# Two-layer hybrid diffusion trunk: the latent query rows of the first two head pairs ahead of the key and query rows of the last two

## The chip, the cores and the metric

The kernel runs on one core of one Trainium2 chip. The metric is the device time of one execution in microseconds (us); lower is better. The core has TensorE (PE, matrix products, with its weight loads PEld), VectorE (DVE), ScalarE (ACT), GpSimd (POOL) and SyncE (SP), which issues the transfers of this kernel. PSUM is the memory that TensorE writes, SBUF the working memory; weights and inputs come from the chip's main memory.

## The reference

Two layers work on 640 tokens: 512 latent ones and 128 context ones. In each layer the modulated input goes through one input projection, whose columns feed three mixers side by side; one output projection merges them, and a SwiGLU channel mixer follows. Cut to what matters here, for the latent tokens:

```python
proj = einsum("bsd,de->bse", h, w_in)
a_x, a_b, a_c, d_q, d_k, d_v, m_cq, m_ckv, m_kpe = split(proj, offs)

y_a = a_b * short_conv(a_c * a_x, conv_w)

sc = einsum("bhmqd,bhmkd->bhmqk", q, k_all) * DIFF_SCALE     # 4 heads, 2 maps each
p  = softmax(sc);  a = p[:, :, 0] - lam * p[:, :, 1]
o_b = rms_norm(a @ v_all, diff_norm_w) * (1 - lam_init)

cq  = rms_norm(m_cq, q_norm_w)                # 384 wide
ckv = rms_norm(m_ckv, kv_norm_w)              # 256 wide
qc  = cq @ w_uq                               # 8 heads: 64 without and 32 with rotation
kv  = ckv_all @ w_ukv                         # 8 heads: 64 of key, 64 of value
k_m = concat([kv[..., :64], kpe_all]);  q_m = concat([q_nope, q_pe])
o_c = softmax(q_m @ k_m.T * MLA_SCALE) @ kv[..., 64:]

y = concat([y_a, y_b, y_c]) @ w_out
```

Latent tokens attend to 512 latent and 128 cached keys, context tokens to the 128 context keys. The keys, values and compressed latents of the context are outputs too.

## The kernel before

Activations lie with features on the partitions and the 640 tokens along the free axis. Every matrix product of the projections is made in three passes: operands are split into a rounded part `hi` and a remainder `lo`, and `matmul3` (L349 in the profile) adds hi by hi, hi by lo and lo by hi. Each 128-row weight block is loaded by SyncE into a staging tile `stg`, and split by ScalarE (L138, cast) and VectorE (L140, subtraction) into one of four weight tiles `wu`; the next split begins when an earlier block is given back (`W.done`). The order of the blocks is fixed by `plan`, from `WIN` for the input projection and from `JOBS` for the latent products.

A layer runs through `stage_in` (the input projection, one job per 128 output rows, in the order of `WIN`, ending with cq0, cq1 and cq2), `attention` (the latent projections and both attentions), the output projection and the channel mixer.

*Jobs.* `attention` walks through `JOBS` in order. `k0` to `k3` (`k_job`, L1131) make the latent key rows of head pairs 0 to 3, 12 matmuls each, and store them to the scratch tensors `kd` and `pd` by three DMAs. `v0` to `v5` (`v_job`) make the values of six key tiles, 6 matmuls each. `e0` and `e1` (`qpe_job`) make the rotated query rows of four heads each, `q0` to `q3` (`q_job`, L1154) the other query rows of a head pair, 18 matmuls each, stored to `qd` and `pd`. k and v jobs read the normalised key latent `ckvn`, e and q jobs the normalised query latent `cq`. A head pair's tiles come together in main memory: `load_pair(p)` (L1174) issues nine DMAs that read the 96 rows of each of the two heads back as `mq` and `mk` (hi and lo), and the context part `p32`.

*Score steps.* `plan_steps` (L1382) lists 64 score steps per layer. The first 32 are the differential attention: two head groups by two halves of the queries by eight steps of one map. The last 32 are the latent attention: four head pairs by two halves by four steps. A step is one call of `scores` (L1188): the matmuls (L1194), VectorE's row maximum `nm` (L1198), ScalarE's exponential `P` with its sum (L1209), VectorE's reciprocal, and GpSimd's scaling (L1228, L1248) or VectorE's weighted difference (L1232). Some steps later the transposes (L1269) and value products (L1280) of the unit follow, one key tile at a time. `STEPS` says how many steps are run in and behind each job of the input projection, and `JSTEPS` for each latent job: a pair is (steps in the middle of the job, steps behind it). `self.g` counts the steps, and other work is hung on the count: `LOADS` gives the counts at which `load_pair(0)` to `load_pair(3)` are issued, `SIDE` and `ASM` place the context attention, the norms and the differential tiles. Steps that no job takes run after the last one, with the latent steps, in the stage "tr".

*Buffers.* In the stage "score", from job dq1 to the end of the latent jobs, PSUM holds two tiles "mm" for projections and one tile "sc" for scores. In the stage "tr", scores use the "mm" tiles and two tiles "trx" take transposes. The probability tile of a step is chosen by `PAT` (for step numbers below `CKS`) or `PATC`: "P" is a pool of 6 that exists only inside `attention` (before that such a tile comes from the shared pool), "t" the shared pool of 31 tiles of 128 by 640, "c" the pool "ck" of 5 that also holds `ckvn`. The shared pool also holds `mk`, `mq`, the differential tiles `dqp` and `dkp`, `cq` and all passing tiles of the k, e and q jobs.

*Deferred work.* The normalisation of `cq` (`norm_cq` L967, `rms_later` L798) is counted in jobs: its statistics (L805, then ten small VectorE instructions) are written behind the third job from cq2 on, its broadcast (L815), the products (L975) and the splits (L836, L837) two jobs later.

```python
for (kind, j), n in zip(JOBS, JSTEPS):
    n = n if isinstance(n, tuple) else (0, n)
    self.mid, n = n
    if kind == "v":
        n += self.mid
    kinds[kind](l, int(j))
    self.tick()
    self.step(n)
```

The program is laid out by a scheduler that places instructions by the written order and by its own timing of when they can run, takes a free buffer for each new tile, and fixes the order on each engine. On the chip each engine follows that order.

Of the kernel before, what the change touches and what calls it, by code (L numbers as in the profile page):

```python
# [54 lines left out]
OUTI = 4  # L55
ADV = 0
HOLD = 2
LOADS = (29, 37, 43, 52)
SIDE = ((34, 37), (37, 40, 43), (36, 40), (47, 50, 56), (44, 47), (49, 51), (51, 54), (60, 62))
ADA_N = 12  # L60
ADA_IN = 1
# [3 lines left out]
ADA_FF2 = 1  # L65
ADA_LAG = 3
LAG = 4
STEPS = {"dv": (1, 2, 1, 1, 1), "ckv0": (0, 1), "ckv1": (0, 2), "ac1": (0, 2), "ab1": (0, 2), "cq0": (0, 2), "cq1": (0, 1), "dk1": (0, 0), "dq1": (0, 0)}
PAT = "PPPt"
PATC = "Pc"  # L70
CKS = 30
NP = 6
JOBS = "k0 k1 k2 k3 v0 v1 v2 v3 v4 e0 v5 e1 q0 q1 q2 q3".split()
JSTEPS = ((0, 1), (0, 1), (0, 1), (3, 0), (0, 1), (1, 0), (0, 0), (0, 0), (0, 1), (0, 2), (0, 0), (0, 0), (0, 1), (0, 0), (2, 1), (1, 0))
ASM = (9, 15)


# [121 lines left out]
class Trunk:  # L199
# [206 lines left out]
    def plan(self):  # L406
# [11 lines left out]
        for l in range(DEPTH):  # L418
# [8 lines left out]
            seen = []  # L427
            for kind, j in JOBS:
                key = {"k": ("uk", l, int(j) // 2), "v": ("uv", l), "e": ("uqpe", l), "q": ("uqn", l, int(j) // 2)}[kind]
# [550 lines left out]
    def dv_job(self, l):  # L980
# [8 lines left out]
        for j in (2, 0, 1, 3, 4):  # L989
# [18 lines left out]
            self.tick()  # L1008
            self.step(STEPS["dv"][j])

# [27 lines left out]
    def stage_in(self, l):  # L1038
# [41 lines left out]
        for n in names[nskew:]:  # L1080
# [4 lines left out]
            else:  # L1085
                u = self.W.get((n, l))
                mid, end = STEPS.get(n, (0, 0))
                ps = self.job(lambda k, p: u[:, p, 128 * k:128 * k + 128], h, NK, "AB", mid)
# [99 lines left out]
    def scores(self, pairs, qc):  # L1188
# [11 lines left out]
        n = self.np - 1  # L1200
        where = PAT[n % len(PAT)] if n < CKS else PATC[n % len(PATC)]
        if where == "c":
# [179 lines left out]
    def plan_steps(self, l):  # L1382
# [7 lines left out]
        def put(step, *fs):  # L1390
            self.after.setdefault(step, []).extend(fs)
# [35 lines left out]
        for g, i in enumerate(ASM):  # L1427
            put(i, lambda g=g: self.assemble_diff(1, 2 * g, 2 * g + 2))
        for p, i in enumerate(LOADS):
            put(i, lambda p=p: self.load_pair(p))  # L1430
# [20 lines left out]
    def attention(self, l):  # L1451
# [7 lines left out]
        kinds = {"k": self.k_job, "v": self.v_job, "e": self.qpe_job, "q": self.q_job}  # L1459
        for (kind, j), n in zip(JOBS, JSTEPS):  # L1460
            n = n if isinstance(n, tuple) else (0, n)
# [252 lines left out]
```

## Time and profile before

| | us |
|---|---|
| median of 3 runs | 1756.45 |
| lowest, highest | 1756.1, 1757.79 |
| profiled execution, its time | 1756.95 |
| its span in the trace | 1755.2 |
| TensorE busy | 1698.5 (97%) |
| VectorE, ScalarE, GpSimd busy | 975.0, 614.1, 247.7 |

The span is the time from the first to the last recorded instruction; the execution takes 1.75 us more. Busy time is the union of an engine's instructions; a busy TensorE can still work at a lower granted clock (1.00 is 2.4 GHz, 0.50 is 1.2 GHz). Layer 0's latent jobs run from about 184 to 238 us and its latent attention to about 350 us; layer 1's from about 1044 to 1098 us and to about 1199 us. A row of the timeline gives the start, the duration, the engine, the line, what is written and read, and in square brackets how long the engine stood idle before and what ended it. A row of the chain is a piece of the chain of work that ended last: start, duration, engine and line.

### The profile page before, as it was taken

To read this page: it belongs to the slowest core of one execution; us is meant where nothing else is said; L and a number is where in the kernel's file an instruction comes from. 1 tells how busy PE (TensorE), PEld (TensorE's weight loads), DVE (VectorE), ACT (ScalarE), POOL (GpSimd) and SP (SyncE) were. 2 spreads that over 40 slices of the span, in tenths; PEclk is the share of its full clock that TensorE was granted. 3 is DMA by queue.
4 is the path that set the end of the run, shared out by engine and by line. 5 is a ranking of instruction groups with operands and counts; after the bars stand their busy time and mean duration, and the time that the engine had idled before them with its cause. 6 is when DMAs were issued, how large, how long until landed. Compare 5 with 4: busy or idle time off the path is not lost.

```text
span 1755.2 us, 29477 instructions
## 1 busy us (share of the span) xinstructions
PE 1698.5 (97%) x11983; PEld 1589.4 (91%) x11983; DVE 975.0 (56%) x1824; ACT 614.1 (35%) x1046; POOL 247.7 (14%) x226
## 2 busy tenths in 40 slices
PE   7999989999999999999999999899999999999997
PEld 6998867698999999999999997678999999999997
DVE  3656777747466656756476668774652233232236
ACT  1334555524432122122245546553353212212221
POOL 0011113440001010101211111332200000000014
PEclk9999989999999999999999999899999999999998
DMA  9665584321355545545314634622212222222211
GB/s 323 210 208 142 169 252 139 119 89 51 94 153 151 156 126 145 174 133 146 107 52 148 217 121 157 173 76 75 73 61 77 81 72 73 73 78 78 68 53 60
DMA packets 100871, 217.38 MB, mean 124 GB/s; under 512 B 12160, under 2 KB 28928, under 8 KB 100736
## 3 DMA queue, kind: packets, MB, share of 16 engines
q1 hardware_dynamic: 100736, 215.50, 39.7%
q8 instruction: 94, 1.54, 0.4%
q14 instruction: 41, 0.34, 0.1%
HBM read 185.28 MB, written 30.18 MB: 123 GB/s over the span
## 4 chain that ended last, share of the span: by engine, by line
PE 86%; DVE 5%; ACT 3%; DMA 2%; issue 2%; POOL 0%; SPq 0%; POOLq 0%; ACTq 0%; DVEq 0%
PE mm L349 61%; PE mm L1194 4%; PE mm L372 4%; PE ac L1280 3%; PE mm L1513 3%; PE trx L1269 3%; PE mm L994 2%; PE mm L401 1%; DMA rawt<-in_w_ada 1%; ACT hv L781 1%; PE ac L476 1%; ACT wu L138 1%; DVE wu L140 1%; PE tr L449 1%; DMA mk<-kd 1%
## 5 line engine op out<-in xcount | busy, mean ns | idle before, releaser
L349 PE MATMUL mm<-h,wu 128*128 128x384 f32 (+1 forms) x4944 | 734.6, 309 | 1.8 <-ACT kp L908 1.5
L349 PEld LDWEIGHTS mm<-h,wu 128*128 128x128 f32 x4944 | 723.3, 188 | 8.7 <-issue 5.3
L138 ACT CAST wu<-stg 128x1024 fp32r<-128x1024 f32 (+2 forms) x200 | 201.5, 1011 | 686.1 <-PE mm L349 333.0
L140 DVE TENSOR_TENSOR wu<-stg,wu 128x1024 fp32r<-128x1024 f32 (+2 forms) x200 | 239.3, 1199 | 155.9 <-ACT wu L138 153.6
L349 PE MATMUL mm<-gh,wu 128*128 128x256 f32 (+1 forms) x1184 | 258.6, 309 | 0.0
L349 PEld LDWEIGHTS mm<-gh,wu 128*128 128x128 f32 x1184 | 198.7, 188 | 0.9 <-issue 0.6
L349 PE MATMUL mm<-gl,wu 128*128 128x384 f32 (+1 forms) x592 | 182.8, 309 | 0.0
L1198 DVE TENSOR_REDUCE nm<-mm 128x1 f32<-128x640 f32 x128 | 104.7, 818 | 50.4 <-PE mm L1194 49.6
L1547 DVE TENSOR_TENSOR gs<-gs,mm 128x640 f32<-128x640 f32 (+2 forms) x48 | 36.6, 763 | 154.2 <-PE mm L349 149.4
L668 DVE SCALAR_TENSOR_TENSOR x<-mm,ga,x 128x512 f32<-128x512 f32 x48 | 35.9, 749 | 145.6 <-PE mm L349 145.6
L349 PEld LDWEIGHTS mm<-gl,wu 128*128 128x128 f32 x592 | 111.4, 188 | 0.2 <-issue 0.2
L527 DVE SCALAR_TENSOR_TENSOR acc<-rawt,scT,acc 128x512 f32<-128x512 f32 x98 | 74.7, 763 | 60.4 <-DMA rawt<-in_w_ada 59.0
L372 PE MATMUL mm<-h,wu 128*128 128x384 f32 (+1 forms) x576 | 99.5, 331 | 7.4 <-ACT h L782 7.1
L372 PEld LDWEIGHTS mm<-h,wu 128*128 128x128 f32 x576 | 92.2, 205 | 12.6 <-ACT h L782 10.2
L349 PE MATMUL mm<-hi,wu 128*128 128x384 f32 (+1 forms) x400 | 89.9, 311 | 0.1
L687 POOL TENSOR_TENSOR accS<-x 128x640 f32<-128x640 f32 x4 | 9.9, 2488 | 507.3 <-DVE x L674 494.7
L1194 PE MATMUL mm<-mk,mq 96*128 96x384 f32 (+1 forms) x384 | 75.0, 336 | 5.2 <-ACT P L1209 2.4
L532 DVE SCALAR_TENSOR_TENSOR rawt<-rawt,scT 128x512 f32<-128x512 f32 x98 | 74.7, 762 | 2.1 <-POOL rawt L525 2.1
L1194 PEld LDWEIGHTS mm<-mk,mq 96*128 96x128 f32 x384 | 63.7, 200 | 12.3 <-ACT P L1209 5.2
L349 PEld LDWEIGHTS mm<-hi,wu 128*128 128x128 f32 x400 | 68.0, 188 | 2.6 <-issue 1.5
L1209 ACT ACTIVATE P<-mm,nm 128x640 f32<-128x640 f32 x56 | 44.6, 797 | 55.7 <-DVE nm L1198 45.0
L525 POOL TENSOR_SCALAR acc<-rawt,scT 128x512 f32<-128x512 f32 x14 | 9.8, 697 | 376.2 <-PE tr L542 376.1
(272 smaller groups left out, 2251.8 us busy)
## 6 DMA issues: line engine op xcount, KB each, us to landing
stg<-in_w_ff SPq DMA_DIRECT2D x104, 512.0 KB, 3.6
rawt<-in_w_ada SPq DMA_DIRECT2D x160, 256.0 KB, 3.1
stg<-in_w_in SPq DMA_DIRECT2D x30, 512.0 KB, 4.4
stg<-in_w_ff SPq DMA_DIRECT2D x32, 448.0 KB, 3.3
raw<-in_w_ada SPq DMA_DIRECT2D x32, 256.0 KB, 6.2
stg<-in_w_out SPq DMA_DIRECT2D x16, 512.0 KB, 4.4
mk<-kd SPq DMA_DIRECT2D x32, 240.0 KB, 5.8
mq<-qd SPq DMA_DIRECT2D x32, 192.0 KB, 5.4
```

Of the source, the lines that this page charges most:

```text
L138: nc.scalar.copy(u[:, 0, :ncol], t[:, :ncol])
L140: (nc.gpsimd if self.lo_pool else nc.vector).tensor_sub(u[:, 1, :ncol], t[:, :ncol], u[:, 0, :ncol].bitcast(F32))
L349: self.last = nc.tensor.matmul(out, w(k, pw), x(k, px), start=(k == 0 and i == 0), stop=(k == nk - 1 and i == 2)).ins
L372: self.last = nc.tensor.matmul(ps, u[:, pw, 128 * k:128 * k + 128], x(k, px)[:, c0:c1], start=(k == 0 and i == 0), stop=(k == NK - 1 and i ...
L527: nc.vector.scalar_tensor_tensor(self.acc[0], w, c[0], self.acc[0], ALU.mult, ALU.add)
L532: nc.vector.scalar_tensor_tensor(self.acc[1], w, c[1], self.acc[1], ALU.mult, ALU.add)
L1194: nc.tensor.matmul(ps[:, 128 + c0:128 + c1], q[:96, qc:qc + 128], k[:96, c0:c1], start=(i == 0), stop=(i == len(pairs) - 1))
L1198: nc.vector.tensor_reduce(nm, s, axis=AX.X, op=ALU.max, negate=True)
L1209: self.exp_end = nc.scalar.activation(P, s, AF.Exp, bias=nm, accum_out=sm).ins
L1269: nc.tensor.transpose(p[:, 256 * i + 128 * q:256 * i + 128 * q + 128], tiles[i, q][:, 128 * kt:128 * kt + 128], self.ident)
L1280: nc.tensor.matmul(acc[64 * i:64 * i + 64, :256], v(kt, i), hold[kt][:, 256 * i:256 * i + 256], start=(kt == 0), stop=(kt == 4))
L1513: self.last = self.nc.tensor.matmul(ps[:, c0:c1], u[:, pw, 128 * k:128 * k + 128], x(k, px)[:, c0:c1], start=(k == 0 and j == 0), stop=(k ...
```

## The change

Five constants change; no function does. The jobs are put in another order, with q0 and q1 ahead of k2, k3, q2 and q3, and e0, e1 among the v jobs. By `plan` the weight block of k2 and k3 comes behind those of v, e and of q0 and q1. Of the 32 differential steps 18 instead of 16 lie in the input projection (one more behind cq1, one behind cq2), and the other 14 are put one behind a job, none behind v1 and v4, and none in the middle of a job. The loads of the first head pair move from step count 29 to 28, which is now reached behind k2 and was reached in the middle of q2. `CKS` moves from 30 to 32, so that step number 31 takes its tile from the shared pool.

```diff
-LOADS = (29, 37, 43, 52)
+LOADS = (28, 37, 43, 52)
...
-STEPS = {"dv": (1, 2, 1, 1, 1), "ckv0": (0, 1), "ckv1": (0, 2), "ac1": (0, 2), "ab1": (0, 2), "cq0": (0, 2), "cq1": (0, 1), "dk1": (0, 0), "dq1": (0, 0)}
+STEPS = {"dv": (1, 2, 1, 1, 1), "ckv0": (0, 1), "ckv1": (0, 2), "ac1": (0, 2), "ab1": (0, 2), "cq0": (0, 2), "cq1": (0, 2), "cq2": (0, 1), "dk1": (0, 0), "dq1": (0, 0)}
...
-CKS = 30
+CKS = 32
...
-JOBS = "k0 k1 k2 k3 v0 v1 v2 v3 v4 e0 v5 e1 q0 q1 q2 q3".split()
-JSTEPS = ((0, 1), (0, 1), (0, 1), (3, 0), (0, 1), (1, 0), (0, 0), (0, 0), (0, 1), (0, 2), (0, 0), (0, 0), (0, 1), (0, 0), (2, 1), (1, 0))
+JOBS = "k0 k1 v0 v1 v2 e0 v3 e1 q0 v4 q1 v5 k2 k3 q2 q3".split()
+JSTEPS = ((0, 1), (0, 1), (0, 1), (0, 0), (0, 1), (0, 1), (0, 1), (0, 1), (0, 1), (0, 0), (0, 1), (0, 1), (0, 1), (0, 1), (0, 1), (0, 1))
```

## Rows read from the trace of the kernel before

**Rows 1.** Busy time by stretch: from and to, length, engines, granted clock, DMA share, GB/s.
```profile
184.00:238.00 54.00, 52.26 (x349) 43.11 (x351) 44.22 (x89) 34.06 (x66) 6.76 (x7) 1.00 0.58 183
238.00:260.00 22.00, 16.45 (x109) 11.68 (x108) 14.82 (x31) 10.75 (x21) 3.54 (x5) 0.77 1.02 294
245.00:249.00 4.00, 3.91 (x13) 3.52 (x14) 2.04 (x6) 0.92 (x3) 0.80 (x1) 0.50 1.04 311
260.00:345.00 85.00, 83.08 (x699) 59.87 (x699) 63.66 (x154) 45.12 (x98) 33.39 (x38) 1.00 0.48 142
1044.00:1098.00 54.00, 52.70 (x324) 43.46 (x320) 45.87 (x91) 36.10 (x69) 6.48 (x7) 1.00 0.47 159
1098.00:1113.00 15.00, 9.32 (x32) 7.17 (x32) 10.60 (x20) 7.99 (x16) 2.57 (x4) 0.66 1.00 300
```

**Rows 2.** TensorE's waits from 238 to 260 us: total, times, longest.
```profile
PE mm L1194 <- ACT P L1209: 4.4, 2, 2.5
```

**Rows 3.** TensorE's waits from 1098 to 1113 us.
```profile
PE mm L1194 <- ACT P L1209: 3.7, 2, 1.9
PE mm L1194 <- DMA mk<-kd: 1.6, 3, 0.8
```

**Rows 4.** Timeline of TensorE at the end of layer 0's latent jobs.
```profile
239.04 0.56 PE L1194 MATMUL mm<-dkp,dqp 96*128 96x384 f32 x2
...
242.06 0.56 PE L1194 MATMUL mm<-dkp,dqp 96*128 96x384 f32 x2 [1.89 <-ACT P L1209]
245.09 0.90 PE L1194 MATMUL mm<-dkp,dqp 96*128 96x384 f32 x2 [2.47 <-ACT P L1209]
245.79 3.75 PE L1194 MATMUL mm<-mk,mq 96*128 96x384 f32 x12
```

**Rows 5.** Timeline of SyncE's issues: q0's last store, first and last of eight loads.
```profile
232.77 0.52 SPq L279 DMA_DIRECT2D qd<-lo x1
...
236.40 0.54 SPq L279 DMA_DIRECT2D mq<-qd x1
...
240.65 1.50 SPq L279 DMA_DIRECT2D mk<-kd x1
```

**Rows 6.** DMA issues from 235 to 243 us: count, size, median us to landing.
```profile
mk<-kd SPq DMA_DIRECT2D x4, 240.0 KB, 6.3
```

**Rows 7.** Timeline of ScalarE: the weight cast and q0's evacuation.
```profile
227.39 1.04 ACT L138 CAST wu<-stg 128x1024 fp32r<-128x1024 f32 x1 [4.64 <-PE mm L349]
...
230.12 0.70 ACT L1162 ACTIVATE mqs<-mm 128x640 f32<-128x640 f32 x1
```

**Rows 8.** Chain that ended last, from 180 to 300 us.
```profile
187.34 2.28 PE mm L349 x12
...
203.95 0.69 PE mm L815 x5
...
206.87 0.29 PE mm L1194 x2
207.17 4.15 PE mm L349 x18
...
220.56 2.65 PE mm L349 x18
223.21 0.44 PE tr L1269 x4
223.65 0.58 PE ac L1280 x4
...
237.54 0.81 POOL P L1228
...
238.73 4.52 DMA mk<-kd
```

**Rows 9.** Timeline of TensorE, layer 0: statistics of the query latent.
```profile
195.12 1.17 PE L805 MATMUL tr<-first,sqr 128*128 128x2 f32 x10
```

**Rows 10.** Timeline of VectorE, layer 0: its last low parts.
```profile
209.78 1.55 DVE L837 TENSOR_TENSOR lo<-raw,hi 128x640 fp32r<-128x640 f32 x2
```

**Rows 11.** Timeline of TensorE, layer 1: the same statistics.
```profile
1049.68 1.17 PE L805 MATMUL tr<-first,sqr 128*128 128x2 f32 x10
```

**Rows 12.** Timeline of VectorE, layer 1: the same low parts.
```profile
1066.67 2.28 DVE L837 TENSOR_TENSOR lo<-raw,hi 128x640 fp32r<-128x640 f32 x3
```

## The prediction

> **What bounds the kernel now.** I first read the busy time by stage [rows 1]. TensorE works nearly all the time wherever matrix products are to hand: 52.26 of 54 us while layer 0 makes its latent key, value and query rows (184 to 238 us), 83.08 of 85 us in the latent attention that follows (260 to 345 us), 52.70 of 54 us in layer 1's projections. The two stretches between are the exception: 22 us with 16.45 us busy at a mean granted clock of 0.77, and 15 us with 9.32 us busy at 0.66. At full clock that work is about 16.45 x 0.77 = 12.7 us and 9.32 x 0.66 = 6.2 us, so the transitions waste about 9.3 and 8.8 us, 18.1 us in all. This is an estimate, since the clock is a mean over the stretch and not over the busy part alone.
>
> Next I read what TensorE waits for there. Layer 0: 4.4 us for the exponentials of the score steps [rows 2]. Layer 1: 3.7 us for the same, and 1.6 us for the loads of the key tiles `mk` [rows 3]. The timeline shows why [rows 4]: the last three differential score steps stand at 239.04, 242.06 and 245.09 us with almost nothing between. While the projections last, scores have one PSUM tile of their own (tag "sc"), so a step waits until the exponential of the step before has read it: 3.02 us from step to step. In the written order of before, 16 of the 32 differential steps lie among the sixteen latent jobs, four of them at q2 and q3, so three are left over when the matrix products end. The first latent scores follow at 245.79 us, 12 matmuls in 3.75 us, at a granted clock of 0.50, which is 1.2 GHz [rows 1].
>
> Behind this stands a second wait. The loads for the first head pair are issued from 236.40 to 240.65 us [rows 5] and take about 6.3 us to land [rows 6], so the last arrive near 247 us. They can't go earlier, because q0's rows were stored only at 232.77 us; its evacuation ran on ScalarE at 230.12 us, behind a weight cast for which ScalarE had sat idle for 4.64 us [rows 7].
>
> **The change, part by part.** No arithmetic and no transfer is added or removed; orders and buffers change.
>
> *Weights.* The second half of `w_uk` is staged behind `w_uqn`'s first half: one DMA, one cast and one subtraction move. Ten jobs lie between k1, which frees the buffer, and k2, which needs them: about 27 us of cover by the prices below. Cost nothing; without that cover k2 would wait for a load, a cast and a subtraction.
>
> *Two score steps* leave the latent jobs for the jobs cq1 and cq2 of the input projection. Their matmuls (0.29 us a step, [rows 8]) cost the same there; their VectorE, ScalarE and GpSimd parts go along. Those jobs hold 48 matmuls each, so two steps of 3.02 us fit. The probability tiles of these two steps come from the shared pool of 31 buffers instead of the attention's own. The step limit 30 to 32 moves the tile of one step, the 32nd, from the "ck" pool to the same shared pool.
>
> *The remaining 14 steps* go one to a job, with none at v1 and v4. TensorE's work between first and last is about 53 us, 3.8 us a step against the 3.02 us that a step needs. So only the last step, behind q3, should be exposed. What stays: one wait of 3.02 less the 0.56 us of its own matmuls, 2.5 us a layer. Gain: 9.3 - 2.5 = 6.8 and 8.8 - 2.5 = 6.3, together 13.1 us. If the steps still bunch up, 0; if nothing stays exposed, 18.1.
>
> *The loads* (four `mq`, four `mk`, one `pd`) are issued one step earlier in the count and much later in the jobs: behind k2, with k3, q2, q3 and three steps to go. By the chain's pieces a k job is 2.28 us, a q or e job 2.65 us, three v jobs 4.15 us [rows 8]; a step with its share of transposes and value products I put at 0.93 us (0.29, and five eighths of the 0.44 + 0.58 us that one key tile takes). That is 2.28 + 5.30 + 2.8 = 10.4 us for 4.3 us of issuing and 6.3 us of flight: just covered, the first head's tiles early. From q0's end to the first latent score there are now 15.4 us of jobs and six steps, about 21 us. Before, q0's end at 223.21 us was followed by its last store at 232.77 us; less the 4.64 us of ScalarE's wait that is 4.9 us, with 3.6 us to the first load, 4.3 of issuing and 6.3 of flight 19.1 us. Covered too, but narrowly. On SyncE, k3's three stores and those of q2 and q3 (three each) are now queued behind the nine loads. They are wanted by the third and fourth pairs' loads, at steps 43 and 52, more than 30 us later: nothing. First-half loads of `w_out` behind them are wanted after attention: nothing.
>
> The load's price weighs a second way. The trace has 6.3 us for a 240 KB key tile [rows 6]. The Trainium skill, DMA: Bandwidth & Descriptors, section "Anatomy of one DMA", gives a fit of 2.0 us plus the bytes at 436 GB/s (for the GpSimd path), about 2.6 us here as an estimate. By it the loads would land inside the score steps, and only the 13.1 us of the steps would count, as they do in my sum; the trace's 6.3 us makes the earlier issue a condition of that gain.
>
> *The order of jobs* has a price, in front of e0. e0 and the q jobs need the normalised query latent. Its statistics are still written behind k1 and its broadcast two jobs later. Before, five v jobs stood between the broadcast and e0; now one does. The chain from statistics to the last low part runs from 195.12 us [rows 9] to 211.33 us [rows 10], 16.2 us, and in layer 1 from 1049.68 [rows 11] to 1068.95 us [rows 12], 19.3 us, most of it queueing on VectorE. The written order now covers v0 to v2 (4.15 us), three steps (2.8) and the broadcast (0.7), 7.6 us. So up to 8.6 and 11.7 us could be uncovered, 20.3 us. The lower bound is 0: v3, v4, v5, k2 and k3 (8.7 us, and four steps, 3.7) can be taken ahead, since instructions are laid out by a timed scheduler. That it does so is in the trace: the statistics, written behind k1, ran at 195.12 us behind all four k jobs. VectorE also has two k evacuations fewer in that stretch. Hence near the low end: 2 us a layer, 4 us. The bound below nothing: the 1.74 and 1.30 us of idle time in the projections [rows 1] could go.
>
> **Sum.** 13.1 - 4 = 9 us faster. The profiled execution took 1756.95 us, 1755.2 us of them its span; the median of the runs is 0.5 us lower, so 1756.45 - 9 = 1747.5 us.
>
> **Rivals.**
> - *Slower: e0 stalls.* TensorE waits ahead of e0 in both layers. For it: the chain is longer than its written cover. Against: the reordering seen in rows 9. It decides from 6.5 us of bubble a layer on, where the gain is eaten. With the full 20.3 us: 1756.45 - 13.1 + 20.3 = 1763.5 us. What an idle TensorE costs beside the gap itself is in the transitions: clock 0.77 and 0.66 there, 1.00 in the stages around [rows 1]. The Trainium skill, TensorE: Matmul & The Clock Gate, Part 1, says the array falls to half clock when it has been idle and gets the full clock back only after sustained work; by that rule a bubble ahead of e0 is paid for again in slow matmuls, some 2 us a layer (an estimate: half of the 3.75 us in rows 4), and this rival would read about 1767 us. The trace agrees with the direction.
> - *Same: the scheduler undoes it.* If v3 to v5, k2 and k3 are all taken ahead of e0, then q0 runs as late as before and the loads too; only one step less is left over in each layer. Gain one wait of 2.5 us a layer at most, often less: about 1753.5 us.
> - *Same: tiles run out.* At the loads the shared pool holds 2 value tiles, 2 outputs, 6 to 8 differential tiles, 6 of the query latent, a probability tile kept from step 16, 3 of k2 and the 8 loaded: 28 to 30 of 31, and k3 wants 3. The chain of before runs through such a wait: GpSimd's last use of a tile at 237.54 us, then the load of `mk` from 238.73 us [rows 8]. If evacuations wait for tiles, 3 to 5 us a layer go again: about 1755 us.
>
> **How the numbers follow.** Forecast 0.54, alone 1740 to 1752 us. e0 stalls 0.20, scheduler 0.14, tiles 0.12. A measurement of this kernel can tell about 0.2%, 3.5 us, from no change. The forecast lies wholly beyond it. Of the stall 0.18 is slower, 0.02 same; of the scheduler 0.04 faster, 0.10 same; of the tiles 0.04 faster, 0.06 same, 0.02 slower. Together faster 0.62, same 0.18, slower 0.20. The range goes from 1738 us (18.1 us of transitions gained) to 1762 us, near the end of the stall rival.
>
> **What would show it.** Right: in the profile after, no run of three differential steps 3 us apart behind q3; TensorE's wait for exponentials and for `mk` at the transitions under 2 us; the mean clock there above 0.9; the first loads of `mq` issued before q3's matmuls. Wrong: an idle TensorE of more than 5 us ahead of the first e job, released by VectorE's low parts; k2 and k3 standing ahead of e0; SyncE or ScalarE waiting for tile releases in the last 15 us of the projections.

## The result and the profile after

**The change made the kernel slower: 1773.2 us, median of runs between 1767.48 and 1785.72, against 1757.11 us; ratio 1.0093, 95% interval 1.0071 to 1.0115.** The forecast was 1747.5 us and its range ended at 1762. The profiled execution took 1773.18 us, 1771.4 of them its span, against 1756.95 and 1755.2 before: 16.2 us to be found. The busy time of each engine on the page after:

```profile
PE 1709.0 (96%) x11983; PEld 1597.0 (90%) x11983; DVE 977.7 (55%) x1824; ACT 613.2 (35%) x1046; POOL 245.0 (14%) x226
```

The same 11983 matmuls, 16.2 us later. To find the place I cut the span at the first matmul of k0 and the first latent score (`mm<-mk`) of each layer. From the one to the other layer 0 took 62.2 us before and takes 69.6; layer 1 took 58.5 and takes 65.2. That is 14.1 of the 16.2 us. Of the rest, 1.8 us lie ahead of layer 0's k0 and 1.9 between layer 0's first latent score and layer 1's k0; 1.6 come back behind layer 1's first latent score. So most of the loss is inside the latent jobs. I cut these once more, at the last matmul of q3. Busy time by stretch of the kernel before (columns as in [rows 1]), jobs and then what is left of the steps, layer 0 and layer 1:

```profile
183.62:237.96 54.34, 52.60 (x352) 43.45 (x354) 44.22 (x89) 34.30 (x66) 6.72 (x7) 1.00 0.58 183
237.96:245.79 7.83, 3.48 (x42) 2.17 (x43) 6.08 (x12) 5.25 (x9) 0.84 (x2) 0.88 0.96 254
1044.43:1097.61 53.18, 51.97 (x319) 43.20 (x319) 45.59 (x89) 35.64 (x68) 6.09 (x7) 1.00 0.47 160
1097.61:1102.89 5.28, 1.55 (x7) 1.03 (x6) 4.53 (x8) 4.75 (x9) 0.68 (x2) 0.78 0.92 246
```

The same of the changed kernel, each with the 15 us behind it, which answer to the transitions of [rows 1]:

```profile
185.41:254.17 68.76, 62.53 (x404) 49.91 (x403) 49.21 (x100) 36.70 (x71) 6.40 (x8) 0.93 0.58 182
254.17:254.96 0.79, 0.29 (x2) 0.03 (x1) 0.46 (x1) 0.75 (x2) 0.00 (x0) 1.00 1.06 252
254.96:269.96 15.00, 12.41 (x58) 8.80 (x60) 10.63 (x21) 7.32 (x15) 3.30 (x4) 0.77 0.94 299
1055.49:1119.86 64.37, 56.91 (x323) 47.56 (x323) 49.83 (x96) 38.12 (x74) 6.06 (x8) 0.92 0.46 149
1119.86:1120.65 0.79, 0.29 (x2) 0.03 (x2) 0.46 (x1) 0.76 (x2) 0.33 (x1) 1.00 1.03 401
1120.65:1135.65 15.00, 11.61 (x60) 8.21 (x60) 10.80 (x23) 7.32 (x15) 3.44 (x5) 0.89 1.04 312
```

Read the two fences against each other. The tail of steps behind q3 is gone as forecast: 7.83 and 5.28 us became 0.79 and 0.79, a gain of 11.5 us. But the jobs themselves take 14.4 and 11.2 us longer, 25.6 us. Four parts of that can be read: TensorE's idle time (length less busy) rose from 1.74 and 1.21 us to 6.23 and 7.46, 10.7 us; the granted clock fell from 1.00 to 0.93 and 0.92, which over 62.53 and 56.91 us of work is an estimated 8.9 us; more of the steps lie there, 29 and 31 score matmuls where there were 26 and 27 (next fences; two a step), three and a half steps at the prediction's 0.93 us, 3.3 us; and layer 0's jobs hold 80 matmuls of the modulation's weights (`rawt`, L449), a side task of TensorE, where there were 36, 2.4 us more. That makes 25.3 us of 25.6.

What TensorE was idle for stands in the groups of line 1194, the score matmuls, in the same stretches of jobs: forms and count, and under them the idle time ahead with its releaser. A step at the stretch's edge may be cut, and a few records can be missing. The kernel before, layer 0 and layer 1:

```profile
L1194 PE MATMUL mm<-dkp,dqp x26: 276/310/446, 185.7 to 235.0; 96*128 96x384 f32 x13, 96*128 96x256 f32 x13
...
L1194 PE MATMUL mm<-dkp,dqp x27: 274/337/442, 1046.5 to 1097.5; 96*128 96x384 f32 x14, 96*128 96x256 f32 x13
  ACT Pt L1209: 0.2, 1
```

The changed kernel:

```profile
L1194 PE MATMUL mm<-dkp,dqp x29: 276/345/689, 188.8 to 254.0; 96*128 96x384 f32 x15, 96*128 96x256 f32 x14
  ACT P L1209: 3.5, 3
  ACT Pt L1209: 0.5, 1
...
L1194 PE MATMUL mm<-dkp,dqp x31: 278/341/689, 1057.6 to 1119.7; 96*128 96x384 f32 x16, 96*128 96x256 f32 x15
  ACT Pt L1209: 4.2, 3
  ACT P L1209: 3.1, 2
```

4.0 and 7.3 us ahead of scores, each released by the exponential of the step before; the kernel before had none and 0.2 us there, and its 4.4 and 3.7 us [rows 2, 3] in the tail. **The wait did not go; it moved into the jobs and grew.** Over the length of the jobs a step now comes every 4.7 and 4.2 us (14.5 and 15.5 steps in 68.76 and 64.37 us), more than the 3.02 us that it needs. Why does TensorE wait even so? Because the steps do not come evenly. These are the nine scores of the two stretches that it waited for, in us:

| score at | distance from the score before | wait | other time of TensorE in that distance |
|---|---|---|---|
| 194.70 | 3.41 | 2.26 | 1.15 |
| 221.56 | 4.63 | 0.46 | 4.17 |
| 224.66 | 3.10 | 0.74 | 2.36 |
| 249.21 | 2.46 | 0.45 | 2.01 |
| 1060.23 | 2.65 | 1.61 | 1.04 |
| 1089.46 | 5.86 | 1.47 | 4.39 |
| 1092.49 | 3.03 | 0.68 | 2.35 |
| 1108.58 | 3.42 | 1.09 | 2.33 |
| 1111.61 | 3.03 | 2.47 | 0.56 |

Seven of the nine stand 2.5 to 3.4 us behind the score before them: these steps took about as long as the 3.02 us measured in the tail, and TensorE had only 0.6 to 2.4 us of work to lay beside them. They make 9.3 of the 11.2 us. Elsewhere 5 to 9 us pass from one score to the next. **The steps are spread over the jobs on the average, but not one by one.** The worst place is a run of three steps in layer 1, between the matmuls of k3 and those of q2; TensorE in the changed kernel:

```profile
1105.16 0.56 PE L1194 MATMUL mm<-dkp,dqp 96*128 96x384 f32 x2
...
1108.58 0.56 PE L1194 MATMUL mm<-dkp,dqp 96*128 96x384 f32 x2 [1.09 <-ACT Pt L1209]
1111.61 0.90 PE L1194 MATMUL mm<-dkp,dqp 96*128 96x384 f32 x2 [2.47 <-ACT P L1209]
1112.31 0.53 PE L349 MATMUL mm<-hi,wu 128*128 128x384 f32 x1
```

It looks like the tail of before [rows 4], now inside the jobs. TensorE has no matmul of a job between 1104.21 and 1112.31 us, because k2 and k3 hold both "mm" tiles. ScalarE takes up k2's evacuation (`mkh`) only behind a weight cast that waits for k3:

```profile
1104.24 1.04 ACT L138 CAST wu<-stg 128x1024 fp32r<-128x1024 f32 x1 [2.45 <-PE mm L349]
...
1108.43 0.68 ACT L1144 CAST mkh<-mm 128x640 fp32r<-128x640 f32 x1
```

It ends with a copy at 1111.46 to 1111.72 us, and then q2 begins. Layer 0 has the same gap, from 236.85 to 243.36 us, and there the profile names the wait for k2's last copy (`mkp`), 1.1 us.

In the other two of the nine, both behind e0, the chain itself was longer. The one in layer 1, on TensorE, VectorE and ScalarE:

```profile
1083.60 0.46 PE L1194 MATMUL mm<-dkp,dqp 96*128 96x384 f32 x2
...
1089.46 0.56 PE L1194 MATMUL mm<-dkp,dqp 96*128 96x384 f32 x2 [1.47 <-ACT Pt L1209]
```

```profile
1084.10 0.82 DVE L1198 TENSOR_REDUCE nm<-mm 128x1 f32<-128x640 f32 x1
...
1086.37 0.95 DVE L140 TENSOR_TENSOR wu<-stg,wu 128x768 fp32r<-128x768 f32 x1
1087.24 0.68 DVE L831 TENSOR_TENSOR qpe<-qpe,sh 128x512 f32<-128x512 f32 x1
```

```profile
1088.00 0.62 ACT L844 CAST hi<-qpe 128x512 fp32r<-128x512 f32 x1 [2.83 <-DVE qpe L831]
1088.53 0.79 ACT L1209 ACTIVATE Pt<-mm,nm 128x640 f32<-128x640 f32 x1
```

The row maximum is ready at 1084.92, but the exponential starts at 1088.53. Ahead of it in ScalarE's order stands the cast of e0's rotated rows, and that waits 2.83 us for VectorE, which does the row maximum, a copy and a weight subtraction before it ends the rotation. The next score needs the one PSUM tile and waits; but most of the 5.86 us was covered, and 1.47 us was lost.

What a bubble costs beyond itself is in layer 0's front. TensorE behind k1:

```profile
191.29 0.55 PE L1194 MATMUL mm<-dkp,dqp 96*128 96x384 f32 x2
...
194.70 0.90 PE L1194 MATMUL mm<-dkp,dqp 96*128 96x384 f32 x2 [2.26 <-ACT P L1209]
195.39 2.13 PE L805 MATMUL tr<-first,sqr 128*128 128x2 f32 x10
```

The granted clock of what follows, in the columns of [rows 1]:

```profile
194.70:201.36 6.66, 6.66 (x21) 5.80 (x22) 4.75 (x17) 2.33 (x6) 0.80 (x1) 0.50 0.93 307
```

Before, the statistics took 1.17 us [rows 9]; behind the 2.26 us of idleness they take 2.13, at a granted clock of 0.50, which is 1.2 GHz, and the value jobs' matmuls 0.63 us where they take 0.39 from 201.91 us on, at 1.00. The Trainium skill's rule quoted in the prediction (TensorE: Matmul & The Clock Gate, Part 1: half clock after idleness) agrees with this.

The loads of layer 0, in SyncE's timeline:

```profile
244.28 0.86 SPq L279 DMA_DIRECT2D mq<-qd  x1
...
249.21 0.43 SPq L279 DMA_DIRECT2D mk<-kd  x1
```

They start ahead of q3's matmuls (250.05 us), as forecast, and 10.7 us ahead of the first latent score (254.96 us) where it was 9.4 [rows 4, 5]. With a median of 5.9 us of flight the last lands near 255 us, and TensorE waits for none of them; in layer 1 it waits 0.3 us for `mk`.

### The profile page after: what moved, and what is told of

The parts are those of the page before. It is cut to its first block, busy times and chain, and to the rows that moved or that the text cites. A ratio compares the mean times of both kernels' runs of the same rounds, so it can differ in the third digit from the quotient of the medians.

```text
span 1771.4 us, 29464 instructions
## 1 busy us (share of the span) xinstructions
PE 1709.0 (96%) x11983; PEld 1597.0 (90%) x11983; DVE 977.7 (55%) x1824; ACT 613.2 (35%) x1046; POOL 245.0 (14%) x226
## 4 chain that ended last, share of the span: by engine, by line
PE 86%; DVE 6%; ACT 4%; issue 2%; DMA 1%; POOL 0%; POOLq 0%; SPq 0%; ACTq 0%; DVEq 0%
PE mm L349 61%; PE mm L1194 4%; PE mm L372 4%; PE ac L1280 3%; PE mm L1513 3%; PE trx L1269 3%; PE mm L994 2%; PE mm L401 1%; PE ac L476 1%; DVE wu L140 1%; ACT hv L781 1%; ACT wu L138 1%; DVE nm L1198 1%; DMA rawt<-in_w_ada 1%; PE tr L449 1%
## 5 line engine op out<-in xcount | busy, mean ns | idle before, releaser
L349 PE MATMUL mm<-h,wu 128*128 128x384 f32 (+1 forms) x4944 | 737.7, 310 | 1.8 <-ACT kp L908 1.5
L349 PEld LDWEIGHTS mm<-h,wu 128*128 128x128 f32 x4944 | 726.4, 189 | 8.7 <-issue 5.3
L138 ACT CAST wu<-stg 128x1024 fp32r<-128x1024 f32 (+3 forms) x200 | 201.6, 1012 | 684.6 <-PE mm L349 333.3
L140 DVE TENSOR_TENSOR wu<-stg,wu 128x1024 fp32r<-128x1024 f32 (+3 forms) x200 | 239.4, 1200 | 154.0 <-ACT wu L138 151.7
L349 PE MATMUL mm<-gh,wu 128*128 128x256 f32 (+1 forms) x1184 | 258.5, 309 | 0.0
L349 PEld LDWEIGHTS mm<-gh,wu 128*128 128x128 f32 x1184 | 198.7, 188 | 0.9 <-issue 0.6
L349 PE MATMUL mm<-gl,wu 128*128 128x384 f32 (+1 forms) x592 | 182.8, 309 | 0.0
L349 PEld LDWEIGHTS mm<-gl,wu 128*128 128x128 f32 x592 | 111.3, 188 | 0.2 <-issue 0.2
L349 PE MATMUL mm<-hi,wu 128*128 128x384 f32 (+1 forms) x400 | 92.3, 318 | 1.1 <-ACT mkp L1146 1.1
L349 PEld LDWEIGHTS mm<-hi,wu 128*128 128x128 f32 x400 | 70.1, 194 | 3.7 <-ACT mkp L1146 1.8
L349 PE MATMUL mm<-lo,wu 128*128 128x384 f32 (+1 forms) x200 | 63.3, 317 | 0.0
```

What stands on the lines that cost most here:

```text
L138: nc.scalar.copy(u[:, 0, :ncol], t[:, :ncol])
L140: (nc.gpsimd if self.lo_pool else nc.vector).tensor_sub(u[:, 1, :ncol], t[:, :ncol], u[:, 0, :ncol].bitcast(F32))
L349: self.last = nc.tensor.matmul(out, w(k, pw), x(k, px), start=(k == 0 and i == 0), stop=(k == nk - 1 and i == 2)).ins
```

## Experiments

Ratios are to the kernel before, with their 95% intervals. "Stretch" is from k0's first matmul to the first `mm<-mk`, layer 0 | layer 1, in the profiled execution: 62.2 | 58.5 us before, 69.6 | 65.2 after.

### One half of the change each

**Order alone** (before, with the new `JOBS`; each job keeps its steps) and **steps alone** (before, with the new `STEPS`, `CKS`, `LOADS` and the new number of steps for each job):

```diff
-JOBS = "k0 k1 k2 k3 v0 v1 v2 v3 v4 e0 v5 e1 q0 q1 q2 q3".split()
+JOBS = "k0 k1 v0 v1 v2 e0 v3 e1 q0 v4 q1 v5 k2 k3 q2 q3".split()
```

> Before, with the new job order alone: each job keeps the score steps that it had before (16 in the input projection, three in k3, three around q2), the loads stand at 29, the step limit at 30. Theory A (late keys: k2 and k3 behind v5 hold both projection tiles of PSUM through three evacuations each on crowded engines, so q2 and q3 wait): the loss is in the order, at least 10 us slower than before, about 1768 us. Theory C (the loss is in the score steps: two moved ahead, the rest spread): the time goes back to that of before, 1757 us within 4 us. Theory B (the shared pool of 31 tiles runs out at the loads): 5 to 10 us slower, since the loads come a step later.

> Before, with the steps alone: old job order, but 18 steps in the input projection, each job's steps as in the changed kernel, loads at 28, step limit 32. Theory A: no loss, 1747 to 1757 us, since what was forecast of the steps (the transitions lose less) is no longer eaten by late keys. Theory C: 10 to 16 us slower than before. Theory B: slower by 5 us or more, because the loads now come behind q0 and hold eight tiles for longer.

Measured: the order alone 1768.14 us, 1.0061 [1.0039, 1.0083], stretch 68.0 | 65.5. The steps alone 1761.71 us, 1.0028 [1.0016, 1.0039], stretch 63.7 | 63.3. Together 10.6 + 4.2 us, about the whole loss. Neither half is a gain, also not the steps in the old order, on which the forecast's 13.1 us rested. The order alone fits theory A's time; the steps alone fit none of the three, 4.2 us slower where A had no loss, B 5 us or more and C 10 to 16.

### Late keys, tiles, single blocks in the queues

**Keys first**: the changed kernel, with k2 and k3 back behind k1 and the query rows still early.

```diff
-JOBS = "k0 k1 v0 v1 v2 e0 v3 e1 q0 v4 q1 v5 k2 k3 q2 q3".split()
+JOBS = "k0 k1 k2 k3 v0 v1 v2 e0 v3 e1 q0 v4 q1 v5 q2 q3".split()
```

> The changed kernel with k2 and k3 put back behind k1, all else kept: q0 and q1 stay ahead of v5, q2, q3, the steps spread one to a job. Theory A: most of the loss goes, 1750 to 1760 us. Theory B: no better than the changed kernel, 1768 us or more, as the loads come earlier (behind q1). Theory C: 1768 us or more.

**32 tiles**: the changed kernel, with one buffer more in the shared pool (`bufs=31` to `bufs=32`).

> The changed kernel with 32 tiles in the shared pool in place of 31, nothing else. Theory B: the exponential that waited for a tile at 240.01 us no longer waits, at least 4 us of the 16 come back, 1769 us or less. Theory A: within 3 us of the changed kernel, 1770 to 1776 us.

Measured: keys first 1769.29 us, 1.007 [1.0049, 1.0091], stretch 72.4 | 62.2; 32 tiles 1773.42 us, 1.009 [1.0064, 1.0115]. The pool of tiles costs nothing: with one buffer more the time is the same. Theory A asked for 1750 to 1760 us of keys first, so by the time the late keys are not the main cause; but the run does not clear them. In layer 0 its stretch holds a wait that the changed kernel hasn't got there, for the modulation's weights, whose transfers are issued behind the loads of the first pair; TensorE's wait from 185.45 to 257.89 us:

```profile
PE tr L449 <- DMA rawt<-in_w_ada: 6.9, 2, 5.7
```

Layer 1 has no such wait, and there the stretch is 3.0 us shorter than in the changed kernel (62.2 for 65.2). The gap of 8.1 us between k3 and q2 is gone there, but one of 7.2 us stands between the k and v jobs. The part of the late keys stays open.

**Weights late**: the buffers of v5's and k3's weights and of `w_uqn` are given back behind q3, which was meant to move the casts of later weights out of these stretches; the same in the kernel before (v5, e1, q1), meant to remove the 4.64 us of ScalarE's wait [rows 7].

```diff
-        if j == 5:
-            self.W.done()
...
-        if p % 2:
-            self.W.done()
+        if p == 3:
+            for _ in range(4):
+                self.W.done()
```

> The changed kernel with the weight buffers of v5, q1 and k3 given back only behind q3, so that no w_out block is cast on ScalarE or subtracted on VectorE between the last latent jobs. Theory H (a queue is blocked: casts and subtractions of weights stand in the fixed order of ScalarE and VectorE ahead of exponentials and evacuations; at 236.89 us the cast that waits 2.54 us for k3's end stands ahead of k2's own evacuation): at least 5 us of the 16 come back, 1768 us or less. Theory P (the two late k jobs hold PSUM, whoever stands in the queue): within 3 us of the changed kernel. The blocks have the whole latent attention, some 100 us, to be split later, so no loss of it is expected.

> The kernel before with the weight buffers of v5, e1 and q1 given back only behind q3. Theory H: the cast that waited 4.64 us at 227.39 us with q0's evacuation behind it is gone, so the loads of the first pair go earlier and the transitions lose less: 3 to 8 us faster than before. Theory P: the same as before within 3 us.

**Deferred splits** (`DEFER = (1, 1, 0)`, meant to issue the splits and stores of e's and q's rows a job later) and **split on GpSimd** (`W_POOL = True`: low parts of the weights move from VectorE to GpSimd during the jobs), both on the changed kernel.

> The changed kernel with the split of the e and q rows written one job later, so that the exponential of the step behind e0 needn't stand behind the cast that waits for e0's rotation on VectorE (2.83 us of ScalarE's idle time at 1088.00 us). Theory H: 3 to 6 us faster than the changed kernel, 1767 to 1770 us. Theory P: no difference beyond 3 us.

> The changed kernel with the subtractions of the weight splits of the latent jobs on GpSimd in place of VectorE (GpSimd is busy 6.4 of 70 us there). Theory V (VectorE, busy about 50 of 65 us in the latent jobs, is what the steps queue for): 4 us or more faster than the changed kernel. Theory H without V: within 3 us, since ScalarE's queue is unchanged.

Measured: weights late 1771.02 us, 1.0073 [1.0054, 1.0091]; in the kernel before 1758.84 us, 1.0003 [0.9993, 1.0012]. Deferred splits 1768.79 us, 1.0063 [1.0048, 1.0078]. Split on GpSimd 1771.17 us, 1.0077 [1.006, 1.0094]. The first two edits don't do what they were meant to do. ScalarE, the kernel before with the weights late, and the changed kernel with deferred splits:

```profile
228.79 1.05 ACT L138 CAST wu<-stg 128x1024 fp32r<-128x1024 f32 x1 [4.64 <-PE mm L349]
```

```profile
1081.33 0.62 ACT L844 CAST hi<-qpe 128x512 fp32r<-128x512 f32 x1 [2.83 <-DVE qpe L831]
```

The 4.64 us and the 2.83 us that they aimed at are still there, and in the stretches from k0 to the first latent score ScalarE and VectorE run the same instructions in the same order as without the edits. For the weights, the scheduler puts the later-written casts back where they were. For the splits, `self.tick()`, which follows each job at once, counts the 1 down to 0, so they are written in the same place. These runs test no block. They say instead how far medians of one order lie apart: 1773.2, 1773.42 (32 tiles), 1771.02 and 1768.79 us, 4.6 us. Deferred splits land inside theory H's 1767 to 1770 us by this spread alone.

The split on GpSimd does move the subtractions, and layer 1's step of 5.86 us behind e0 is gone with it. TensorE's waits for exponentials in layer 1's jobs are 6.1 us even so, where they were 7.3. The time is 2 us lower, within the spread, as theory H without V had it; but its layer 0 has 3.8 us of the wait for the modulation's weights.

### The scores' tile, and jobs without steps

**Shared tiles** (`ATT_ANY = True`): during the latent jobs the scores rotate through three PSUM tiles together with the jobs, in place of the one "sc" tile. On the changed kernel and on the kernel before:

> The changed kernel, with one thing else: during the latent jobs the scores share three PSUM tiles with the jobs in place of one tile of their own. Theory S (the stretch of the jobs is as long as the chain of differential score steps over their single PSUM tile: score, row maximum, exponentials, next score): the chain is broken, a score can start while the exponentials before it are outstanding, and most of the 14 us lost in the two stretches comes back: stretches of 60 to 64 us, time 1757 to 1763 us. Rival J (the jobs themselves take longer in the new order, by late weights and evacuations, whatever the steps do): stretches of 67 to 70 us as before this edit, time 1769 to 1775 us. Against both: the jobs lose their own second tile at times, which can cost some us.

> The kernel before, with the scores of the latent jobs on the three shared PSUM tiles. Theory S: the old order's stretches (62.2 and 58.5 us) hold 27.5 and 25.4 us of waits of the chain as well, part of which comes back: time 1748 to 1756 us. Rival J: nothing hangs on the scores' tile, time within 3 us of before (1754 to 1760 us), or later by what the jobs lose with the shared tiles.

**No steps** among the jobs (every entry of `JSTEPS` is (0, 0)), in the new and in the old order:

> The changed kernel with no score steps laid among the latent jobs (they all run behind the last job). The time itself gets longer in any case, as steps and jobs no longer overlap. Theory S: the order of jobs has no price of its own, so the stretch from the first k matmul to the last q matmul is as long as in the old order without steps, within 1.5 us a layer, and the time within 3 us of it. Rival J: it is longer by some 5 us a layer, and the time by 8 to 12 us.

> The kernel before with no score steps among the latent jobs, as the mate of the run above. Theory S: the same time as it within 3 us. Rival J: 8 to 12 us faster than it.

Shared tiles, changed kernel: 1764.11 us, 1.0032 [1.0018, 1.0045], 9 us of the loss back, 1 us outside what theory S had named. TensorE's waits of more than 0.7 us for exponentials in its jobs, two in layer 0 and two in layer 1:

```profile
PE mm L349 <- ACT Pt L1209: 1.7, 1, 1.7
PE mm L349 <- ACT P L1209: 0.8, 1, 0.8
...
PE mm L349 <- ACT P L1209: 2.0, 1, 2.0
PE mm L349 <- ACT Pt L1209: 1.7, 1, 1.7
```

Scores now wait 0.2 us and none, where they waited 4.0 and 7.3 in the changed kernel. But the jobs' own matmuls (L349) wait for exponentials in their place, since they share the tiles: 2.7 and 3.7 us of such waits are left in all. The busy time by stretch of the same run, jobs of layer 0 and layer 1:

```profile
188.05:246.38 58.33, 53.57 (x334) 44.77 (x331) 45.59 (x92) 33.76 (x67) 6.20 (x8) 0.97 0.59 183
...
1052.87:1111.37 58.50, 52.75 (x314) 44.08 (x315) 45.60 (x90) 34.56 (x67) 6.46 (x8) 0.98 0.54 169
```

Clock 0.97 and 0.98 against 0.93 and 0.92, an estimated 6.2 us less lost to it in both layers; idle time 4.8 and 5.8 us against 6.2 and 7.5, 3.2 us less. 58.3 and 58.5 us against 68.8 and 64.4, with 26 and 27 score matmuls in them against 29 and 31, so part of the steps is back in the tail; the stretch is 62.7 | 61.5 us, though layer 0's k0 starts 2.6 us later. One thing the run doesn't separate: the jobs may hold a third tile as well, and layer 1's gap of 8.1 us behind k3 is gone. This is what the Trainium skill, Perfetto Trace Analysis, section "Matmuls", asks for: independent groups of matmuls should rotate through PSUM banks, so that the evacuation of one lies beside the next. The trace agrees for the new order, with these numbers. The old order gains nothing by it: 1760.52 us, 1.0017 [1.0006, 1.0027], against theory S's 1748 to 1756; the waits of 27.5 and 25.4 us that its expectation names are not TensorE's, which waits 4.4 and 3.9 us for exponentials in these stretches, nearly all of it in the tail. Its layer 0 also waits 5.6 us for the modulation's weights, which it did not before.

Without steps both orders are alike: new 1788.77 us, 1.0172 [1.0144, 1.0199], old 1790.5 us, 1.0185 [1.017, 1.0201]. Busy time of the jobs, first k to last q matmul, layer 0 and layer 1; the new order:

```profile
184.26:231.27 47.01, 41.95 (x298) 35.69 (x297) 28.38 (x55) 23.34 (x39) 0.80 (x1) 0.96 0.65 212
...
1061.05:1103.75 42.70, 38.99 (x216) 34.53 (x215) 28.42 (x52) 24.58 (x42) 0.80 (x1) 0.96 0.52 182
```

and the old:

```profile
186.10:234.16 48.06, 41.15 (x296) 36.08 (x295) 26.38 (x49) 22.26 (x36) 0.00 (x0) 0.93 0.70 227
...
1066.95:1107.17 40.22, 36.11 (x213) 32.91 (x213) 26.00 (x45) 23.10 (x38) 0.00 (x0) 1.00 0.58 193
```

47.0 and 42.7 us against 48.1 and 40.2, 1.4 us more in both layers together (2.5 in layer 1, over the bound of 1.5 that theory S had set for a layer). In layer 0 both hold waits for the modulation's weights, 1.7 us in the new order and 3.9 in the old; without these the new order is 3.6 us longer in both. The times compare less well, because the new order keeps 18 steps in the input projection and the old one 16, so that two steps a layer more lie in the old one's tail. With the steps in place and 16 of them ahead in both, the order alone made the stretches 5.8 and 7.0 us longer. **The order of the jobs has a small price of its own, 1.4 to 3.6 us; most of it is paid through the steps between them.** Rival J's 8 to 12 us fall.

### What the rest hangs on

> The changed kernel with the scores on the shared PSUM tiles, and with the splits and stores of e's and q's rows issued one job later. Theory Q (behind the tile, the rest of the loss is blocks in the fixed orders of ScalarE and VectorE, where splits that wait for rotated rows stand ahead of row maxima and exponentials): the 4 to 5 us that the deferral gave by itself come on top of the 9 of the tiles: 1758 to 1761 us. Rival R (both edits heal the same waits, the rest sits elsewhere): 1763 to 1766 us, no better than the shared tiles alone (1764.1).

> As the run above, and the weights of v5, q1 and k3 given back behind q3, so that no cast of later weights stands on ScalarE ahead of an exponential in these stretches. Theory Q: another 2 us, 1756 to 1759 us, level with the kernel before. Rival R: 1762 to 1766 us.

> The kernel before with the splits and stores of e's and q's rows issued one job later. Theory Q, with the blocks as a thing of the new order (there e0, e1, q0, q1 have score steps between them; in the old order the last four jobs have few): within 3 us of before, 1754 to 1760 us. If the blocks cost the old order as well: 1752 to 1754 us.

> The kernel before with the new order of jobs alone, each job keeping its number of score steps, and the scores on the shared PSUM tiles (the order alone was 1768.1 us with the single tile). Theory S: most of its 10.6 us goes with the tile: 1759 to 1763 us. If the places of the steps matter more than the tile: 1765 to 1770 us.

Measured: shared tiles with deferred splits 1761.55 us, 1.0031 [1.0018, 1.0044]; with the weights late as well 1764.82 us, 1.0043 [1.0028, 1.0058]; the kernel before with deferred splits 1759.25 us, 1.0004 [0.9994, 1.0014]; the order alone with shared tiles 1763.47 us, 1.0027 [1.0017, 1.0037]. Since the deferral and the late weights leave the orders of ScalarE and VectorE in these stretches as they were, the first three runs repeat the shared tiles and the kernel before, and agree with them: 1.0031 and 1.0043 against 1.0032, 1.0004 against 1. They decide nothing between theory Q and rival R. The order alone, a real change, loses half of its price to the shared tiles, just over the 1759 to 1763 us of theory S.

### Half as many steps

**Seven steps** a layer among the jobs, behind the same jobs in both orders; `JSTEPS` is (0, 1) for k0, k2, v0, e0, e1, q1 and q2 and (0, 0) for the rest:

> The changed kernel with seven score steps among the latent jobs of a layer in place of 14 (one behind each of k0, k2, v0, e0, e1, q1, q2), the rest behind the last job. Theory S (the new order is dear only while the chain of steps over its one tile is full): from the first k to the last q matmul the new order then takes as long as the old one with the same seven steps, within 2 us a layer, and the two times are within 4 us of each other. Rival H (each step between the new order's jobs meets rows and casts that stand ahead of it on ScalarE and VectorE, full chain or not): the new order is longer by 3 to 4 us a layer and 6 to 8 us in all, half of what it is with 14 steps. Against the kernel before both are slower, as eight steps a layer lie alone.

> The kernel before with the same seven steps behind the same seven jobs, the mate of the run above. Theory S: within 4 us of it. Rival H: 6 to 8 us faster than it.

Measured: new order 1770.26 us, 1.0069 [1.0052, 1.0086]; old 1772.26 us, 1.0083 [1.0068, 1.0098]. The jobs of both layers, new order:

```profile
185.97:242.84 56.87, 51.01 (x351) 42.85 (x349) 39.34 (x79) 30.06 (x56) 3.66 (x5) 0.94 0.58 195
...
1053.77:1107.21 53.44, 46.56 (x270) 40.09 (x269) 39.77 (x75) 31.55 (x59) 3.67 (x5) 0.97 0.44 150
```

and old:

```profile
184.82:238.06 53.24, 49.60 (x341) 40.90 (x339) 35.91 (x72) 28.75 (x52) 3.72 (x4) 0.94 0.68 218
...
1057.25:1104.79 47.54, 43.01 (x258) 37.41 (x257) 35.18 (x68) 29.52 (x54) 3.72 (x4) 1.00 0.49 165
```

By the whole time theory S is right: the orders are within 4 us, the new one 2 us ahead. By the jobs alone it is not: they take 3.6 and 5.9 us longer in the new order, where it had allowed 2, as rival H said. Part of this is count: 16 and 18 score matmuls lie among the new order's jobs, 14 and 14 among the old one's, and the tail is shorter for it, also because the new order keeps two steps a layer more in the input projection. The sum decides the time: stretches of 71.2 | 67.8 us new, 74.4 | 67.6 old.

Half as many steps are not half as dense, though. In the new order's layer 0 the scores stand as with 14 steps up to 217.42 us, and then there is none until 239.75 us. The last one and its exponential:

```profile
217.42 0.57 PE L1194 MATMUL mm<-dkp,dqp 96*128 96x384 f32 x2
```

```profile
236.84 0.80 ACT L1209 ACTIVATE Pt<-mm,nm 128x640 f32<-128x640 f32 x1
```

The exponential runs 19.4 us behind its score, and the one tile is held for so long; the traces do not show why it was placed there. Layer 1 and the old order have such a hole too. So seven steps mean a hole of 22 us near the end of the new order's jobs and one of 23 to 25 us in the midst of the old one's, and neither theory was tested as meant.

Now set the steps against the stretches. From seven steps to the full number the old order goes from 74.4 to 62.2 and from 67.6 to 58.5 us, 21.3 us of gain for nine steps a layer more among the jobs; the new order from 71.2 to 69.6 and from 67.8 to 65.2, about 4 us for seven. **In the new order the added steps are hardly hidden at all.** The times say the same: they are worth 14.8 us in the old order (1772.26 to 1757.48) and nothing in the new one (1770.26, with all steps 1773.2). No version among these runs beats the kernel before.

## Why the prediction was wrong

- *The gain in the tail* was right in kind and nearly in size: 13.1 us forecast, 11.5 seen. No three steps 3 us apart stand behind q3, and TensorE's waits for `mk` are down to 0.3 us, its waits for exponentials in the 15 us behind to 1.1 and 0.7. The clock above 0.9 did not come: 0.77 and 0.89 in the 15 us behind.
- **The step that failed** is the one on the remaining 14 steps: "TensorE's work between first and last is about 53 us, 3.8 us a step against the 3.02 us that a step needs. So only the last step, behind q3, should be exposed." The 3.02 us held: seven of the nine scores that TensorE waited for stand 2.5 to 3.4 us behind the one before. What failed is the 3.8 us, an average of cover that no single step is promised. As the changed kernel was laid out, these seven steps had 0.6 to 2.4 us of TensorE's work beside them, while other scores stood 5 to 9 us apart. The worst run of three lay behind k3, where TensorE had no job matmul for 8.1 us: the prediction priced the late k2 and k3 by their weights alone ("Cost nothing"), and not by the two PSUM tiles that they hold until ScalarE and VectorE have evacuated them. The prediction's own prices showed a part of it: one v job is 4.15 / 3 = 1.4 us, with the step's share of 0.93 us 2.3 us, less than 3.02, and the steps behind v0, v3 and v5 come after no more than that. The longer chain behind e0's rows (4.6 and 5.9 us) was not foreseen either, but cost 1.9 of 11.2 us. So TensorE waited inside the jobs, and then ran them at a lower clock: 25.6 us of longer jobs, where the sum had 4 us. That the steps carry it is shown by the runs without steps, and that 9 us hang on the PSUM tiles by the shared tiles, which give both the scores and the jobs more of them. That the uneven cover is the reason is read from the trace, and no run with an even spread tests it.
- *The price of the order*, a bubble ahead of e0, was the wrong place. The rival "e0 stalls" forecast the right sign, but not this mechanism. e0's matmuls follow a score without a gap; TensorE's timeline after:

```profile
205.94 0.56 PE L1194 MATMUL mm<-dkp,dqp 96*128 96x384 f32 x2
206.33 0.34 PE L349 MATMUL mm<-hi,wu 128*128 128x384 f32 x1
```

- *That a bubble is paid twice* stood in the prediction only beside that rival, at some 2 us a layer. It came to an estimated 4.4 and 4.6 us of clock in the two layers, and belonged in the sum of any case in which TensorE can wait.
- *The scheduler undoes it* falls: k2's matmuls run from 232.39 us, behind e1, q0 and q1. *Tiles run out* falls by the run with 32. Two sums of the prediction are off by 0.1 to 0.2 us, without consequence: the jobs behind q0 add up to 15.3 us, and the stall's time to 1763.65 us.
- *Two steps leave the latent jobs* hardly came true: from k0 to the first latent score the trace has 31 and 33 score matmuls, before 32 and 33.
- *The loads* were right: covered, with no wait for them in layer 0 and 0.3 us in layer 1.
- *The smallest difference to be told*, 3.5 us, was too small for the changed kernel: four medians of its order lie 4.6 us apart.

What stays open: some 6 us that shared tiles don't give back, with latent stretches of 62.7 | 61.5 us; the part of the late keys; and what the blocks in the orders of ScalarE and VectorE cost, as two of the three edits aimed at them moved nothing and the third met another wait.

## What to carry to other kernels

An average of cover hides nothing by itself: for a chain of dependent steps, compare its period with the work between each two steps as they are laid out, not with all the work divided by all the steps. If the chain holds a single PSUM tile, a late link does not only delay itself: here it stopped the engine that was meant to hide it, and then that engine ran at half clock. Before work is spread evenly, vary how much of it is spread (none, half, all), and read in the trace where the steps came to stand. The same holds for any edit of written order under a scheduler: look first whether the engines' orders changed at all.

## What was not expected of the hardware

The mean granted clock does not explain a time across orders. The kernel before with deferred splits had the same mean granted clock as the changed kernel, 0.981, at a span of 1758.7 us against 1771.4; and the changed kernel with 32 tiles had 0.987 at 1766.6 us. In three profiled runs of the old order the span went with it: 1752.7 us at 0.987 (weights late, the same order in these stretches), 1755.2 at 0.985 and 1758.7 at 0.981 (deferred splits); in the changed kernel 0.981 stands beside 1771.4 and 1783.9 us alike. The changed kernel also spreads more from run to run, 1767.48 to 1785.72 us, where the kernel before, over all runs beside the experiments, stays within 1753.84 to 1762.47; the runs don't show why.
